# Group-norm sums with the squares as moving operand: four token tiles on four column groups of 32, then VectorE transposes

## The chip, the cores and the metric

The kernel runs on one core of one Trainium2 chip. The metric is the device time of one execution in microseconds (us), the median of several. Engines are named as in the profile: PE is TensorE's matmuls and PEld its weight loads, DVE is VectorE, ACT is ScalarE, POOL is GpSimd, SP is SyncE, which only issues DMAs here. A matmul has a stationary operand, which is loaded into the array first (PEld), and a moving operand, which streams through it (PE); the output has one partition for each column of the stationary operand.

## The reference, cut to what matters

One hybrid block over 512 tokens of width 1024: a dilated attention and a Mamba-2 mixer side by side, gates, an output projection, and an MLP, all float32. The change is in the grouped RMS norm at the end of the Mamba-2 mixer: 2048 channels in 8 groups of 256, and for each token and group the root mean square over the 256 channels.

```
y = y.reshape(b, s, SSM_INNER) * jax.nn.silu(z)
yg = y.reshape(b, s, SSM_GROUPS, SSM_INNER // SSM_GROUPS)
yg = yg * lax.rsqrt(jnp.mean(yg * yg, axis=-1, keepdims=True) + RMS_EPS)
y = yg.reshape(b, s, SSM_INNER) * norm_w
```

## The kernel before, in words

Tokens are 4 tiles of 128. The input projection, the attention, the Mamba-2 mixer, the output projection and the MLP follow each other; all large products run on PE as three passes of a split float32 (a high part, `hi` or `h`, and a rest, `lo` or `l`, in the type float32r), one matmul with 512 columns each. The weights come in units of 1 MB through two staging buffers (`ws`), and ACT and DVE split each unit into `wh` and `wl` (line 96 and line 99) before PE uses it.

The Mamba-2 mixer takes the 8 channel groups one after the other (`ssm_group`, line 768). Within a group the work is a chain of steps, and between the steps PE gets matmuls of the next units to do: the generator `ssm_group` yields, and the list `SSM_FILL` (line 46) says how many microseconds of projection work (x, B and C, z, and the projection of the group before, `sp`) go between two steps. Each matmul is kept in program order (`mm`, line 226), so the order on PE is that of the code. On DVE and ACT a part of the instructions is kept in order and the others are placed by the scheduler of the tile framework.

The part that the change touches is the end of a group. Channels lie on partitions and tokens along the free dimension, so `y` is two tiles (j = 0, 1) of 128 channels by 512 tokens. ACT squares both (line 841, the factor 1/sqrt(256) makes the sum a mean), DVE adds the two (line 844, into `sq[0]`), and then the sum over the 128 partitions is a matmul: for each token residue c the 128 tokens 4t + c (a column step of 4) are the stationary operand, and the first column of `ones` is the moving operand; the result is column c of `pn` with tokens on partitions (line 850). `rstd_of` adds epsilon on DVE (line 212, `rt`) and POOL raises to the power -1/2 (line 215). `rt` goes to DRAM and comes back spread over all partitions in token order (`rg`, lines 855 and 857, both issued from POOL), and DVE multiplies it in (line 864) to give `yt`, which the projection `sp` of the group needs.

On DVE the instruction `rt` stands among the instructions of the next group's convolution (lines 691 to 697: ACT makes `ch` from `psx`, DVE adds three taps with 511, 510 and 509 columns, ACT makes `ct`), and on ACT these are followed by the decays of the next group (`e` and `w`, lines 761 to 765) and by the split of the z weights (line 96).

Of the kernel before, what the change touches and what calls it, by code (L numbers as in the profile page):

```python
# [11 lines left out]
F32 = mybir.dt.float32  # L12
F32R = mybir.dt.float32r
AF = mybir.ActivationFunctionType
# [4 lines left out]
P = 128  # L19
T = 512  # L20
NT = 4
# [16 lines left out]
UC = 256  # L38
# [45 lines left out]
def hybrid_block(ctx: ExitStack, tc: tile.TileContext, a: dict):  # L84
    nc = tc.nc
    act, dve, pool, pe, sp = nc.scalar, nc.vector, nc.gpsimd, nc.tensor, nc.sync
# [8 lines left out]
    def split(src, hi, lo, eng=None, pinned=False, lo_pinned=False):  # L95
        ins = act.activation(hi, src, AF.Copy)  # L96
        if pinned:
            tc.keep_in_program_order(ins)
        ins = (eng or dve).tensor_tensor(lo, src, hi.bitcast(F32), op=ALU.subtract)  # L99
        if lo_pinned:  # L100
            tc.keep_in_program_order(ins)
# [107 lines left out]
    def rstd_of(dst, ms, ms2=None):  # L209

        if ms2 is None:
            dve.tensor_scalar(dst, ms, EPS, None, ALU.add)
        else:
            dve.tensor_scalar(dst, ms, ms2, EPS, ALU.add, ALU.add)
        pool.tensor_tensor(dst, dst, mhalf.broadcast_to(list(dst.shape)), op=ALU.pow)

    ones = const.tile([P, P], F32, name="ones")
# [5 lines left out]
    def pin(ins):  # L223
        return tc.keep_in_program_order(ins)

    def mm(*args, **kw):
        tc.keep_in_program_order(pe.matmul(*args, **kw))  # L227

    def tr(dst, src):
        tc.keep_in_program_order(pe.transpose(dst, src, ident))  # L230
# [4 lines left out]
    def three(ps, wh, wl, uh, ul, start, stop, w_moving=False):  # L235
        if w_moving:
            mm(ps, uh, wh, start=start, stop=False)
            mm(ps, uh, wl, start=False, stop=False)
            mm(ps, ul, wh, start=False, stop=stop)
        else:  # L240
            mm(ps, wh, uh, start=start, stop=False)
            mm(ps, wh, ul, start=False, stop=False)
            mm(ps, wl, uh, start=False, stop=stop)
# [14 lines left out]
    def abank(name):  # L258
        return psa.tile([P, T], F32, name=name, tag="a")
# [18 lines left out]
    with tc.tile_pool(name="start", bufs=1, reuse_waits="tile") as st:  # L278
# [163 lines left out]
        t = [vp.tile([P, GROUPS, NT, HG], F32, name=f"dt{j}") for j in range(4)]  # L442
# [185 lines left out]
    for key in ATT_UNITS:  # L628
        n, j = key[:-1], int(key[-1])
# [54 lines left out]
    sg = sctx.enter_context(tc.tile_pool(name="ssm", bufs=1, side="right", reuse_waits="tile"))  # L684
# [15 lines left out]
    def bc64(t, g, c0=0, c1=NT):  # L700
        v = t[:, g * 16 + c0 * HG : g * 16 + c1 * HG]
        return v.unsqueeze(2).broadcast_to([P, (c1 - c0) * HG, 64])

    def h64(ap_):
        return ap_.rearrange("p (q e) -> p q e", e=64)
# [62 lines left out]
    def ssm_group(g, sz):  # L768

        xs2 = [convs.pop((g, c)) for c in range(2)]  # L770
        w, e = ws_e.pop(g)

        xd = sg.tile([P, NT * UC], F32, name=f"xd{g}", tag="xd")
        for b in range(2):
            pt = abank(f"ptx{g}_{b}")
            for c2 in range(2):
                c = 2 * b + c2
                for j, xx in enumerate(xs2):
                    tr(pt[:, c2 * UC + j * P : c2 * UC + (j + 1) * P], xx[:, c * P : (c + 1) * P])
            dve.tensor_tensor(h64(xd[:, b * T : (b + 1) * T]), h64(pt), bc64(dtc, g, 2 * b, 2 * b + 2), op=ALU.mult)  # L780
        xs = sg.tile([P, 3 * UC], F32, name=f"xs{g}", tag="prev")
        dve.tensor_tensor(h64(xs), h64(xd[:, : 3 * UC]), bc64(ds_, g, 0, 3), op=ALU.mult)
        xsp = [sg.tile([P, 3 * UC], F32R, name=f"xs{n}{g}", tag=f"xs{n}") for n in "hl"]
        split(xs, *xsp)
        yield

        bt, ct = convs.pop((g, 2)), convs.pop((g, 3))
        pb = abank(f"pb{g}")
        for c in range(3):
            tr(pb[:, c * P : (c + 1) * P], bt[:, c * P : (c + 1) * P])  # L790
        bk = [sg.tile([P, TC], F32R, name=f"bk{n}{g}", tag=f"bk{n}") for n in "hl"]
        split(pb[:, :TC], *bk)
        pcb = abank(f"pcb{g}")
        for c in range(NT):
            cs = slice(c * P, (c + 1) * P)
            mm(pcb[:, cs], bt[:, cs], ct[:, cs], start=True, stop=True)
        cbm = sg.tile([P, NT, P], F32, name=f"cbm{g}", tag="cbm")
        dve.tensor_tensor(cbm, pcb.rearrange("p (c l) -> p c l", c=NT), tri.unsqueeze(1).broadcast_to([P, NT, P]),
                          op=ALU.mult)
        for c in range(NT):  # L800
            wv = w[:, c * HG : (c + 1) * HG, :]
            dve.tensor_tensor(wv, wv, cbm[:, c, :].unsqueeze(1).broadcast_to([P, HG, P]), op=ALU.mult)
        yield

        prev = sg.tile([P, 3, UC], F32, name=f"prev{g}", tag="prev")
        pst = [abank(f"pst{g}_{b}") for b in range(2)]
        for c in range(3):
            pv = pst[c // 2][:, (c % 2) * UC : (c % 2 + 1) * UC]
            bs, us = slice(c * P, (c + 1) * P), slice(c * UC, (c + 1) * UC)
            three(pv, bk[0][:, bs], bk[1][:, bs], xsp[0][:, us], xsp[1][:, us], True, True)  # L810
        with tc.high_priority(offset=200):
            act.activation(prev[:, 0, :], pst[0][:, 0:UC], AF.Copy)
            for c in (1, 2):
                pv = pst[c // 2][:, (c % 2) * UC : (c % 2 + 1) * UC]
                pin(dve.tensor_tensor(h64(prev[:, c, :]), h64(prev[:, c - 1, :]), bc64(cd, g, c, c + 1), op=ALU.mult))
                pin(dve.tensor_tensor(prev[:, c, :], prev[:, c, :], pv, op=ALU.add))
        while held:
            held.pop()()
        yield

        ys, sq = [], []
        pyds = [abank(f"pyd{g}_{j}") for j in range(2)]
        for j in range(2):
            for c in range(NT):
                for half in range(2):
                    h = 2 * j + half
                    mm(pyds[j][64 * half : 64 * half + 64, c * P : (c + 1) * P],
                       xd[:, c * UC + h * 64 : c * UC + (h + 1) * 64], w[:, c * HG + h, :], start=True, stop=True)
        for j in range(2):
            y = sg.tile([P, T], F32, name=f"y{g}_{j}", tag="y", bufs=2)  # L830
            dve.scalar_tensor_tensor(y, xs2[j], dskip[:, 2 * g + j : 2 * g + j + 1], pyds[j], op0=ALU.mult, op1=ALU.add)
            pyo = abank(f"pyo{g}_{j}")
            for c in range(1, NT):
                mm(pyo[:, (c - 1) * P : c * P], prev[:, c - 1, j * P : (j + 1) * P], ct[:, c * P : (c + 1) * P],
                   start=True, stop=True)
            t1 = sg.tile([P, TC], F32, name=f"t1{g}_{j}", tag="t1", bufs=2)
            dve.tensor_tensor(t1, pyo[:, :TC], e[:, j, :], op=ALU.mult)
            dve.tensor_tensor(y[:, P:], y[:, P:], t1, op=ALU.add)
            dve.scalar_tensor_tensor(y, y, 0.5, sz[j], op0=ALU.mult, op1=ALU.mult)
            q = sg.tile([P, T], F32, name=f"sq{g}_{j}", tag="sq", bufs=2)  # L840
            pin(act.activation(q, y, AF.Square, scale=1.0 / math.sqrt(UC)))
            ys.append(y)
            sq.append(q)
        dve.tensor_tensor(sq[0], sq[0], sq[1], op=ALU.add)
        yield

        pn = abank(f"pn{g}")
        by4 = sq[0].rearrange("p (t c) -> p c t", c=NT)
        for c in range(NT):
            mm(pn[:, c : c + 1], by4[:, c, :], ones[:, 0:1], start=True, stop=True)  # L850
        rt = sg.tile([P, NT], F32, name=f"rt{g}", tag="rt", bufs=2)
        rstd_of(rt, pn[:, :NT])

        row = dram.tile([P, NT], F32, name=f"rt_d{g}")
        pool.dma_start(row, rt)
        rstd = sg.tile([P, T], F32, name=f"rg{g}", tag="rg")
        pool.dma_start(rstd, row.rearrange("(o t) c -> o (t c)", o=1).broadcast_to([P, T]))
        if g + 1 < GROUPS:
            decays(g + 1)
        yield  # L860
        yield
        yt = yts[g] = [sg.tile([P, 2, T], F32R, name=f"yt{n}{g}", tag=f"yt{n}", bufs=1) for n in "hl"]
        for j in range(2):
            pin(dve.scalar_tensor_tensor(ys[j], ys[j], nw[:, 2 * g + j : 2 * g + j + 1], rstd,
                                         op0=ALU.mult, op1=ALU.mult))
            split(ys[j], yt[0][:, j, :], yt[1][:, j, :])
# [394 lines left out]
    j = last  # L1261
# [106 lines left out]
```

## Time and profile before

| | |
|---|---|
| time, median of 3 runs | 1097.21 us (1097.13 to 1097.43) |
| the profiled execution, its time | 1096.37 us |
| its span, first to last instruction | 1094.5 us |
| PE busy | 1083.4 us, 99% of the span |
| DVE, ACT, POOL busy | 730.9, 527.9, 72.0 us |
| mean granted TensorE clock | 0.998 of full speed |

A busy PE is an engine with a matmul in it, not one at its peak: matmuls overlap, and a row's length is longer than the step to the next row. What a block of matmuls costs is therefore read from the starts of the rows before and after it.

### The profile page before, as it was taken

How to read it: one execution, taken by the hardware profiler on the slowest of the kernel's cores; microseconds unless marked ns; L12 is line 12 of the kernel's file. 1: busy time of each engine (PE TensorE's matmuls, PEld its weight loads, DVE VectorE, ACT ScalarE, POOL GpSimd, SP SyncE). 2: the span in 40 equal slices, each digit the busy share in tenths (PEclk: the TensorE clock that was granted, in tenths of full speed). 3: DMA queues.
4: the chain of work that ended last, by engine and by line, in shares of the span. 5: the costliest groups of instructions: out<-in, count | busy, mean ns of one | idle time of the engine just before them, and what ended most of it. 6: DMA issues, size and time to landing. Idle time of an engine off the chain costs nothing.

```text
span 1094.5 us, 14714 instructions
## 1 busy us (share of the span) xinstructions
PE 1083.4 (99%) x5959; PEld 929.5 (85%) x5959; DVE 730.9 (67%) x1088; ACT 527.9 (48%) x921; POOL 72.0 (7%) x87
## 2 busy tenths in 40 slices
PE   9999999999999999999999999999999999999997
PEld 8988887778888888888888878889899998888886
DVE  6557666446776879696969695868677886243324
ACT  6256656435374645546373623443467666232322
POOL 3203122000000000000000000000000000000000
PEclk9999999999999999999999999999999999999999
DMA  8232112323333332323324222560233323333202
GB/s 278 81 116 78 55 63 68 106 68 106 116 87 119 84 125 78 125 82 121 112 92 150 86 82 88 191 192 1 78 116 116 102 93 135 116 118 113 80 37 78
DMA packets 87653, 113.06 MB, mean 103 GB/s; under 512 B 4624, under 2 KB 74768, under 8 KB 86560
## 3 DMA queue, kind: packets, MB, share of 16 engines
q1 hardware_dynamic: 85216, 101.01, 28.7%
q0 software_dynamic: 2224, 11.09, 3.0%
q8 instruction: 47, 0.77, 0.3%
q14 instruction: 22, 0.18, 0.1%
q10 hardware_dynamic: 144, 0.00, 0.0%
HBM read 109.92 MB, written 2.18 MB: 102 GB/s over the span
## 4 chain that ended last, share of the span: by engine, by line
PE 95%; DVE 2%; DMA 1%; issue 1%; ACT 1%; SPq 0%; POOLq 0%; POOL 0%; DVEq 0%; ACTq 0%
PE psd L227 15%; PE psx L227 8%; PE psz L227 8%; PE psbc L227 8%; PE pssp L227 7%; PE psuX L227 6%; PE psu L227 4%; PE psga L227 4%; PE psgs L227 4%; PE psk L227 3%; PE psq L227 3%; PE psuZ L227 3%; PE psv L227 3%; PE psap L227 3%; PE psp L227 2%; PE pso L227 2%
## 5 line engine op out<-in xcount | busy, mean ns | idle before, releaser
L227 PE MATMUL psd<-wl_dn,hh 128*128 128x512 f32 x240 | 93.5, 390 | 0.0
L227 PE MATMUL psd<-wh_dn,hh 128*128 128x512 f32 x240 | 93.5, 390 | 0.0
L227 PE MATMUL psd<-wh_dn,hl 128*128 128x512 f32 x240 | 93.5, 389 | 0.0
L99 DVE TENSOR_TENSOR hl<-hidden,hh 128x512 fp32r<-128x512 f32 x31 | 21.1, 692 | 71.3 <-ACT hh L96 71.3
L96 ACT ACTIVATE hh<-hidden 128x512 fp32r<-128x512 f32 x31 | 19.1, 628 | 91.8 <-PE psd L227 91.8
L227 PEld LDWEIGHTS psd<-wh_dn,hh 128*128 128x128 f32 x240 | 45.1, 188 | 9.4
L227 PEld LDWEIGHTS psd<-wl_dn,hh 128*128 128x128 f32 x240 | 45.1, 188 | 9.3
L227 PEld LDWEIGHTS psd<-wh_dn,hl 128*128 128x128 f32 x240 | 45.1, 188 | 9.3
L693 DVE SCALAR_TENSOR_TENSOR ch<-psx,cw,ch 128x511 f32<-128x511 f32 (+2 forms) x48 | 35.9, 747 | 23.0 <-ACT ch L691 22.3
L227 PE MATMUL psz<-uh,wh_z 128*128 128x512 f32 x128 | 51.1, 399 | 0.0
L227 PE MATMUL pssp<-yth,wh_sp 128*128 128x512 f32 x128 | 50.9, 398 | 0.0
L227 PE MATMUL psx<-uh,wl_x 128*128 128x512 f32 x128 | 50.1, 392 | 0.7 <-DVE wl_x L99 0.7
L227 PE MATMUL psx<-uh,wh_x 128*128 128x512 f32 x128 | 50.6, 395 | 0.0
L227 PE MATMUL pssp<-yth,wl_sp 128*128 128x512 f32 x128 | 50.2, 392 | 0.0
L227 PE MATMUL psz<-uh,wl_z 128*128 128x512 f32 x128 | 50.1, 391 | 0.0
L227 PE MATMUL pssp<-ytl,wh_sp 128*128 128x512 f32 x128 | 50.0, 391 | 0.0
L227 PE MATMUL psbc<-uh,wh_bc 128*128 128x512 f32 x128 | 50.0, 390 | 0.0
L227 PE MATMUL psz<-ul,wh_z 128*128 128x512 f32 x128 | 50.0, 390 | 0.0
L227 PE MATMUL psbc<-uh,wl_bc 128*128 128x512 f32 x128 | 49.9, 390 | 0.0
L227 PE MATMUL psbc<-ul,wh_bc 128*128 128x512 f32 x128 | 49.8, 389 | 0.0
L227 PE MATMUL psx<-ul,wh_x 128*128 128x512 f32 x128 | 49.8, 389 | 0.0
L696 ACT ACTIVATE ct<-ch 128x512 f32<-128x512 f32 x32 | 20.0, 626 | 52.1 <-DVE ch L693 52.1
(360 smaller groups left out, 3267.4 us busy)
## 6 DMA issues: line engine op xcount, KB each, us to landing
ws_up<-in_w_up_dram SPq DMA_DIRECT2D x16, 1024.0 KB, 5.5
ws_dn<-in_w_down_dram SPq DMA_DIRECT2D x15, 1024.0 KB, 5.0
ws_z<-in_w_in_dram SPq DMA_DIRECT2D x8, 1024.0 KB, 7.1
ws_x<-in_w_in_dram SPq DMA_DIRECT2D x8, 1024.0 KB, 5.2
w<-acs_d POOLq DMA_DIRECT2D x8, 1024.0 KB, 5.6
ws_bc<-in_w_in_dram SPq DMA_DIRECT2D x16, 512.0 KB, 4.7
ws_sp<-in_w_ssm_proj_dram SPq DMA_DIRECT2D x8, 1024.0 KB, 4.9
ws_ga<-in_w_in_dram SPq DMA_DIRECT2D x4, 1024.0 KB, 5.8
```

The costliest lines, as they stand in the source:

```text
L96: ins = act.activation(hi, src, AF.Copy)
L99: ins = (eng or dve).tensor_tensor(lo, src, hi.bitcast(F32), op=ALU.subtract)
L227: tc.keep_in_program_order(pe.matmul(*args, **kw))
L693: dve.scalar_tensor_tensor(h[:, d:], ps[:, : T - d], cw[:, ct, 3 - d : 4 - d], h[:, d:], op0=ALU.mult, op1=ALU.add)
L696: act.activation(t, h, AF.Tanh)
```

## The change

The squares are written in another order of tokens, and their sum over partitions is taken with the operands exchanged. ACT's square now reads `y` with a step of 4 tokens and writes `q` so that token 128j + 4p + b of the group lies at place 128j + 32b + p. Each matmul c now has 32 columns of `ones` as stationary operand and the 128 contiguous columns of token tile c as moving operand; its output is 32 equal rows, on partitions 32c to 32c + 31 of `pn`. The four matmuls thus use the four column groups of the array. A new DVE instruction transposes `pn` in squares of 32 by 32 into the new tile `pnt` (one more buffer of 512 bytes per partition in the pool `ssm`), so that partition 32c + p, square b, holds the mean of token 128c + 4p + b, and `rstd_of` reads the first column of each square. From `rt` on the layout is the same as before. The DMAs are the same.

```diff
-            pin(act.activation(q, y, AF.Square, scale=1.0 / math.sqrt(UC)))
+
+            pin(act.activation(q.rearrange("n (j b p) -> n j b p", j=NT, b=4),
+                               y.rearrange("n (j p b) -> n j b p", j=NT, b=4), AF.Square, scale=1.0 / math.sqrt(UC)))
...
         pn = abank(f"pn{g}")
-        by4 = sq[0].rearrange("p (t c) -> p c t", c=NT)
         for c in range(NT):
-            mm(pn[:, c : c + 1], by4[:, c, :], ones[:, 0:1], start=True, stop=True)
+            mm(pn[32 * c : 32 * c + 32, :P], ones[:, :32], sq[0][:, c * P : (c + 1) * P], start=True, stop=True)
+        pnt = sg.tile([P, 4, 32], F32, name=f"pnt{g}", tag="pnt")
+        dve.transpose(pnt.rearrange("p b q -> p (b q)"), pn[:, :P])
         rt = sg.tile([P, NT], F32, name=f"rt{g}", tag="rt", bufs=2)
-        rstd_of(rt, pn[:, :NT])
+        rstd_of(rt, pnt[:, :, 0])
```

On PE the place of the four matmuls is the same in all 8 groups; here the third group of channels, between matmuls of the x projection of the next one (`psx`). Before:

```order
L227 MATMUL psx_1_3489<-ul,wh_x_3354 128x512
L227 MATMUL psx_1_3489<-uh,wl_x_3355 128x512
L227 MATMUL pn_3496<-ones,sq_0_3404 128x1 x4
L227 MATMUL psx_1_3489<-uh,wh_x_3354 128x512
L227 MATMUL psx_1_3489<-ul,wh_x_3354 128x512
```

And now:

```order
L227 MATMUL psx_1_3493<-ul,wh_x_3358 128x512
L227 MATMUL psx_1_3493<-uh,wl_x_3359 128x512
L227 MATMUL pn_3500<-sq_0_3408,ones 32x128 x4
L227 MATMUL psx_1_3493<-uh,wh_x_3358 128x512
L227 MATMUL psx_1_3493<-ul,wh_x_3358 128x512
```

Nothing moved; only the form of the four is another. On DVE the same place, from the last step of `y` to the `ct` of the next group. Before:

```order
L839 SCALAR_TENSOR_TENSOR y_1_3406<-y_1_3406,sz_1_3312 128x512
L844 TENSOR_TENSOR sq_0_3404<-sq_0_3404,sq_1_3416 128x512
L693 SCALAR_TENSOR_TENSOR ch_3481<-psx_0_3456,cw,ch_3481 128x511
L212 TENSOR_SCALAR rt_3501<-pn_3496 128x4
L693 SCALAR_TENSOR_TENSOR ch_3481<-psx_0_3456,cw,ch_3481 128x510
L693 SCALAR_TENSOR_TENSOR ch_3481<-psx_0_3456,cw,ch_3481 128x509
L697 SCALAR_TENSOR_TENSOR ct_3486<-ct_3486,ch_3481 128x512
```

And now:

```order
L839 SCALAR_TENSOR_TENSOR y_1_3410<-y_1_3410,sz_1_3316 128x512
L846 TENSOR_TENSOR sq_0_3408<-sq_0_3408,sq_1_3420 128x512
L693 SCALAR_TENSOR_TENSOR ch_3485<-psx_0_3460,cw,ch_3485 128x511
L693 SCALAR_TENSOR_TENSOR ch_3485<-psx_0_3460,cw,ch_3485 128x510
L854 STREAM_TRANSPOSE pnt_3505<-pn_3500 128x128
L693 SCALAR_TENSOR_TENSOR ch_3485<-psx_0_3460,cw,ch_3485 128x509
L212 TENSOR_SCALAR rt_3507<-pnt_3505 128x4
L697 SCALAR_TENSOR_TENSOR ct_3490<-ct_3490,ch_3485 128x512
```

The instruction that waits for `pn` stands one place later: the tap with 510 columns now comes ahead of it, and the transpose between the taps with 510 and 509 columns. It is so in the third to the seventh group. Beside that, in the first group the mask product `cbm` (line 798) comes three places earlier on DVE, and one half of a split of x weights (line 96) four places earlier on ACT. POOL and SP have the same order as before.

## Rows read from the trace of the kernel before

**Rows 1.** The page: part 1 (busy time and share of the span), part 2 (the granted clock in 40 slices), part 4 (the chain that ended last, by engine).

```profile
PE 1083.4 (99%) x5959; PEld 929.5 (85%) x5959; DVE 730.9 (67%) x1088; ACT 527.9 (48%) x921; POOL 72.0 (7%) x87
...
PEclk9999999999999999999999999999999999999999
...
PE 95%; DVE 2%; DMA 1%; issue 1%; ACT 1%; SPq 0%; POOLq 0%; POOL 0%; DVEq 0%; ACTq 0%
```

**Rows 2.** Busy time by stretches, two whole groups, from one sum over partitions to the next; columns as in the head.

```profile
core 0: us, PE busy (x) PEld busy (x) DVE busy (x) ACT busy (x) POOL busy (x), PEclk, DMA share, GB/s
399.26:451.36 52.10, 52.10 (x273) 43.93 (x273) 42.53 (x63) 26.22 (x46) 2.72 (x4) 1.00 0.34 105
451.36:503.46 52.10, 52.10 (x273) 43.93 (x273) 42.53 (x63) 26.22 (x46) 2.73 (x4) 1.00 0.33 108
```

**Rows 3.** PE in order of time around one block of the sums (start us, length us, instruction; equal ones in a row are merged, the length is then that of the whole).

```profile
450.22 0.39 PE L227 MATMUL psx<-ul,wh_x 128*128 128x512 f32 x1
...
451.13 0.40 PE L227 MATMUL psx<-uh,wl_x 128*128 128x512 f32 x1
451.36 1.80 PE L227 MATMUL pn<-ones,sq 128*128 128x1 f32 x8
453.02 0.47 PE L227 MATMUL psx<-uh,wh_x 128*128 128x512 f32 x1
453.34 0.39 PE L227 MATMUL psx<-ul,wh_x 128*128 128x512 f32 x1
```

**Rows 4.** Groups of instructions by line and form (count, then busy us, mean ns of one, idle before).

```profile
L227 PEld LDWEIGHTS pn<-ones,sq 128*128 128x128 f32 x64 | 15.5, 324 | 0.3
L227 PEld LDWEIGHTS pcb<-ct,ct 128*128 128x128 f32 x64 | 7.8, 192 | 0.0
```

**Rows 5.** PE around 32 passes on two column groups of 64 (`pyd`, 16 matmuls), and eight passes on the whole array (`pcb`, 4 matmuls of the same 128 moving columns).

```profile
332.88 1.97 PE L227 MATMUL pyd<-w,xd 128*64 128x128 f32 x32
...
479.55 1.06 PE L227 MATMUL pcb<-ct,ct 128*128 128x128 f32 x8
```

**Rows 6.** The same two and the passes of `po` (the attention's values, also two column groups of 64) by form.

```profile
L227 PE MATMUL pyd<-w,xd 128*64 128x128 f32 x256 | 16.2, 277 | 0.8 <-DVE w L802 0.8
L227 PE MATMUL po<-pT,vtok 128*64 128x384 f32 x24 | 4.9, 486 | 0.0
L227 PE MATMUL po<-pT,vtok 128*64 128x256 f32 x24 | 3.6, 379 | 0.0
L227 PE MATMUL po<-pT,vtok 128*64 128x128 f32 x24 | 2.3, 273 | 0.0
L227 PE MATMUL pcb<-ct,ct 128*128 128x128 f32 x64 | 8.5, 275 | 0.0
```

**Rows 7.** PE around one block of `po` (8 matmuls, 16 passes of 512, 384, 128 and 256 columns, four of each), between matmuls on the whole array.

```profile
139.58 0.39 PE L227 MATMUL psq<-uh,wl_q 128*128 128x512 f32 x1
139.90 2.38 PE L227 MATMUL po<-pT,vtok 128*64 128x512 f32 x16
142.21 0.50 PE L227 MATMUL psq<-uh,wh_q 128*128 128x512 f32 x1
142.54 0.40 PE L227 MATMUL psq<-ul,wh_q 128*128 128x512 f32 x1
```

**Rows 8.** Groups by form: the squares on ACT, and a copy of 128 by 128 from PSUM on DVE.

```profile
L841 ACT ACTIVATE sq<-y 128x512 f32<-128x512 f32 x16 | 10.1, 632 | 70.5 <-DVE y L839 70.3
...
L635 DVE COPY acs<-pc 128x128 f32<-128x128 f32 x1 | 0.3, 290 | 2.9 <-PE pc L227 2.9
```

**Rows 9.** The weight loads of the sums of rows 3 on PE.

```profile
451.13 1.94 PEld L227 LDWEIGHTS pn<-ones,sq 128*128 128x128 f32 x8
```

**Rows 10.** DVE in order of time over the place of rows 3 (in brackets the idle time before and what ended it).

```profile
448.56 0.69 DVE L839 SCALAR_TENSOR_TENSOR y<-y,sz 128x512 f32<-128x512 f32 x1
449.95 0.69 DVE L844 TENSOR_TENSOR sq<-sq,sq 128x512 f32<-128x512 f32 x1 [0.70 <-ACT sq L841]
451.01 0.75 DVE L693 SCALAR_TENSOR_TENSOR ch<-psx,cw,ch 128x511 f32<-128x511 f32 x1 [0.37 <-ACT ch L691]
453.25 0.16 DVE L212 TENSOR_SCALAR rt<-pn 128x4 f32<-128x4 f32 x1 [1.50 <-PE pn L227]
453.33 1.52 DVE L693 SCALAR_TENSOR_TENSOR ch<-psx,cw,ch 128x510 f32<-128x510 f32 x2
```

**Rows 11.** ACT in order of time, from the square to the z weights' split.

```profile
449.29 0.63 ACT L841 ACTIVATE sq<-y 128x512 f32<-128x512 f32 x1 [2.75 <-DVE y L839]
...
454.95 0.63 ACT L696 ACTIVATE ct<-ch 128x512 f32<-128x512 f32 x1 [3.97 <-DVE ch L693]
455.49 1.87 ACT L761 ACTIVATE e<-w 64x384 f32<-64x384 f32 x4
457.38 0.40 ACT L764 ACTIVATE w<-w,acs 128x128 f32<-128x128 f32 x1
457.69 0.76 ACT L691 ACTIVATE ch<-psx,cb,cw 128x512 f32<-128x512 f32 x1
...
466.69 1.04 ACT L96 ACTIVATE wh_z<-ws_z 128x1024 fp32r<-128x1024 f32 x1
```

**Rows 12.** The second half of the z weights' rest on DVE in order of time, and the multiplication by `rg` after it.

```profile
467.76 1.22 DVE L99 TENSOR_TENSOR wl_z<-ws_z,wh_z 128x1024 fp32r<-128x1024 f32 x1 [0.67 <-ACT wh_z L96]
...
469.51 0.74 DVE L864 SCALAR_TENSOR_TENSOR y<-y,nw,rg 128x512 f32<-128x512 f32 x1
```

**Rows 13.** The weight load on PE that is the first to need the half of rows 12.

```profile
469.02 0.19 PEld L227 LDWEIGHTS psz<-uh,wl_z 128*128 128x128 f32 x1
```

**Rows 14.** POOL's issue of the spread of `rt` in order of time.

```profile
457.08 0.55 POOL L857 DMA_DIRECT2D rg<-rt_d  x1 [1.65 <-issue]
```

**Rows 15.** Its time from issue to landing, over all eight groups.

```profile
DMA to landing us min/median/max: 3.3/3.6/3.9
```

## The prediction

> **What bounds the kernel now.** I read the page first [rows 1]: PE has work in 99% of the span, the chain that ended last runs over PE for 95%, and the clock is at its upper level (2.4 GHz) in all slices. So the question is how long PE's own queue is, and where PE waits for something else. Then busy time by stretches [rows 2]: from one sum to the next a group takes 52.10 us, PE has no gap in it, DVE is busy 42.53 us (82%), ACT 26.22 us (50%). The reader is to see that time taken off PE's queue counts in full as long as DVE's and ACT's results still arrive in time, and that DVE has little to spare at single places.
>
> Next, PE in order of time around the sums [rows 3]. Matmuls with 512 columns start 0.2275 us apart (451.13 less 450.22, by 4). From the last one before the sums (451.13) to the second after them (453.34) are 2.21 us, where 2 x 0.2275 = 0.455 would do. The four sums, eight passes in the trace, thus cost 1.755 us per group, 14.04 us in all 8. With one moving column they stream nothing to speak of: the time is weight loads, and a load of the strided squares takes 324 ns, where one of 128 contiguous columns takes 192 [rows 4].
>
> **The change on PE.** It removes those 14.04 us and adds eight passes of 128 moving columns on column groups of 32. No row has groups of 32; two kinds have groups of 64, and I take the price from them.
>
> How many passes run at once: on the whole array the eight passes of `pcb` take 1.06 us less one length of 0.275, so 0.785 / 7 = 0.112 us each. The 32 passes of `pyd` with the same 128 columns take 1.97 - 0.277 = 1.69 us, by 31 is 0.055 us each [rows 5, 6]. Half the step at the same length of a pass: the two column groups run at once.
>
> What entering and leaving costs: the block of `po` takes 142.54 - 139.58 - 0.455 = 2.505 us [rows 7]. A pass grows by 486 - 379 = 107 ns, or 379 - 273 = 106 ns, per 128 columns [rows 6]. Its passes, two at once, are 2 x (512 + 384 + 128 + 256) = 2560 columns one after the other, 20 x 0.107 = 2.14 us. The rest, 0.365 us, is going into the split array and out of it, once per block.
>
> With four groups at once the new block is two rounds of 0.107 us and 0.365 us, together 0.58 us. It saves 1.755 - 0.58 = 1.175 us per group, 9.4 us in 8. If only two run at once it is four rounds, 0.79 us, saving 0.96 us, 7.7 us in all. If none do, eight rounds, 1.22 us, saving 0.53 us, 4.3 us. I take four at once, since `pyd` halves its step with nothing left over.
>
> The Trainium skill has a rule against this: TensorE: Matmul & The Clock Gate, Part 3, "The mechanism", says that matmuls start and end strictly in program order. The trace shows two passes of a matmul each; if those of one column group must follow each other and the next group may not pass them, four groups would overlap only where the second pass of one meets the first of the next. By that rule the sum would be about the case with two at once; by the halved step of `pyd` [rows 5] it is the case with four.
>
> **The square on ACT.** It is the same count of elements, read with a step of 16 bytes. Two squares per group, of 632 ns [rows 8]; the second is on the way to the sums. No row of ACT reads with such a step. The low bound is no change. The nearest row is the weight load with that very step, 132 ns more for 128 columns, so 1.03 ns per element and 0.53 us for 512 [rows 4]; I take this. Does PE see it? The sum of squares on DVE ends at 449.95 + 0.69 = 450.64 and the loads of the sums begin at 451.13 [rows 9, 10], 0.49 us later. Going into column groups moves the first pass further: at `po` it starts 139.90 - 139.58 = 0.32 us after the last matmul, where the step is otherwise 0.2275 [rows 7], so the slack is 0.58 us. Hence nothing at 0.53 us, and in the five groups with this order (the third to the seventh) 5 x (extra - 0.58) beyond. On ACT the second square delays `ch` (450.20, with 0.28 us idle before it), and DVE's first tap by about 0.2 us [rows 10, 11].
>
> SBUF — State Buffer of the Trainium skill, in its note on cachelines, says that a 4-byte read which meets a new 16-byte line each time pays a penalty. The trace agrees for the weight loads (324 against 192 ns [rows 4]); for ACT no run here shows it, and the page gives no figure.
>
> **The transpose on DVE.** Eight more instructions. The nearest row is the copy of 128 by 128 from PSUM, 290 ns [rows 8]; below I allow `rt`'s 160 ns, above the 690 ns of an instruction with 512 columns [rows 10]. I take 0.29 us, 2.3 us on DVE in all. Queued behind it on DVE are the tap with 509 columns, `rt` and `ct`, and ACT waits for these taps. So the place matters. Before, DVE stands 1.50 us waiting for `pn`, until 453.25, and two taps of 1.52 us together come behind it; ACT's `ct` (454.95, 3.97 us idle) follows, and from there ACT works without a gap up to the z weights [rows 10, 11]. Now the tap with 510 columns is done during the wait. The sums end 1.175 us earlier, at about 452.05; the taps with 511 and 510 columns are through at about 452.5 (452.7 with the longer square), the transpose at 452.8 to 453.0, the tap with 509 at 453.5 to 453.7. `ct` starts 1.25 to 1.4 us earlier than before.
>
> **What is late next.** PE reaches psz's low half 1.175 us earlier, and there the slack is 469.02 - (467.76 + 1.22) = 0.04 us [rows 12, 13]: the z weights' split must move forward by as much. Its chain on ACT begins with `ct` (1.25 us earlier) and with `ch` of psx at 457.69, which needs PE, itself 1.175 us earlier. So it follows, with next to nothing over. For the last hundredths, and for the first group's other order on DVE, I charge 0.06 us per group, 0.5 us in all. A transpose of 0.69 us would make that chain 0.2 to 0.3 us late in six groups, 1.5 us more. The spread of the result is covered: `rg` lands at 457.08 + 3.6 = 460.7, and DVE multiplies by it at 469.51 [rows 12, 14, 15]; two DVE instructions more ahead of it (0.29 + 0.75 us) do not reach that. POOL and SP issue the same DMAs in the same order.
>
> **Sum.** 9.4 - 0.5 = 8.9 us less. The profiled execution took 1096.37 us with a span of 1094.5 us and would take 1087.5; the median of the runs lies 0.84 us above it, so I predict 1097.21 - 8.9 = 1088.3 us.
>
> **Rivals.**
> 1. Two column groups at once, for which the rows themselves are the only evidence (no row has four). Saving 7.7 - 0.5 = 7.2 us: 1090.0 us.
> 2. The change doesn't do what it says: groups of 32 do not overlap, eight rounds. 4.3 - 0.5: 1093.4 us. Against it stand both blocks with groups of 64.
> 3. The gain turns into a wait for DVE or ACT: either the transpose takes 0.69 us (1.5 us more, 1089.8 us), or the square takes twice the taken surcharge, 1.06 us, and PE waits 0.48 us in five groups (2.4 us, 1090.7 us). For it speaks that two slacks are 0.04 and 0.58 us; against it that the tap now fills the wait.
> 4. Slower: the array is emptied at each change of column group instead of once per block. Then 0.365 us is paid four times, and with eight rounds the block costs 1.46 + 0.86 = 2.32 us, 0.56 us more than now in each group: 1097.2 + 4.5 = 1101.7 us. It decides from a block above 1.755 us. Against it: `pyd` changes between two groups all the time and shows no such gap.
>
> **Chances.** Forecast 0.58 (its own range 1087.0 to 1089.3), rival 1 0.20, rival 2 0.06, rival 3 0.11, rival 4 0.03; 0.02 for a gain lost wholly in waits, within 0.2%. A measurement of this kernel can tell 0.2%, 2.2 us, from no change. All cases but rival 4 and the last are faster by more: 0.95, 0.02, 0.03. The range 1086.8 to 1091.4 holds the forecast, rivals 1 and 3 and the bounds of square and transpose from below; rivals 2 and 4 are left out.
>
> **What would show it.** In PE's order the step from the last matmul before the sums to the second after them: 1.04 us for four at once, 1.25 for two, 1.68 for none, 2.8 for rival 4. Eight passes of `pn` with starts in two bunches of four. One group to the next in 50.9 us instead of 52.10. The square's mean (0.63 or 1.16 us), the transpose's (0.29 us), the idle of DVE before it, and PE's waits for `sq` and `wl_z`, which are to stay under 0.1 us each. The forecast is wrong if PE shows waits of several tenths there, or if the block's step is above 1.2 us.

## The result and the profile after

| | before | after |
|---|---|---|
| median | 1097.22 us (1097.13 to 1097.43, 4 runs) | 1087.28 us (1086.76 to 1087.56, 4 runs) |
| profiled execution; its span | 1096.37; 1094.5 us | 1087.34; 1085.6 us |

The ratio is 0.9909 (95% interval 0.9891 to 0.9926): 9.9 us less. Parts 1 and 4 of the page after [rows 1]:

```profile
PE 1074.3 (99%) x5959; PEld 915.7 (84%) x5959; DVE 732.2 (67%) x1096; ACT 535.5 (49%) x921; POOL 72.0 (7%) x87
...
PE 92%; DVE 4%; DMA 2%; ACT 1%; issue 1%; SPq 0%; POOL 0%; POOLq 0%; DVEq 0%; ACTq 0%
```

PE still has work in 99% of the span and lost 9.1 us of busy time. DVE gained 1.3 us and ACT 7.6 us, and the time fell all the same. The windows of two whole groups [rows 2]:

```profile
core 0: us, PE busy (x) PEld busy (x) DVE busy (x) ACT busy (x) POOL busy (x), PEclk, DMA share, GB/s
397.45:448.34 50.89, 50.89 (x273) 42.18 (x272) 42.62 (x64) 27.23 (x46) 2.72 (x4) 1.00 0.36 109
448.34:499.24 50.90, 50.90 (x273) 42.18 (x273) 42.64 (x64) 27.23 (x46) 2.72 (x4) 1.00 0.35 109
```

A group takes 50.893 us instead of 52.100, 1.207 less, and PE has no gap in it. Around one block, PE in order of time (start us, length us; equal rows merged) [rows 3]:

```profile
448.03 0.39 PE L227 MATMUL psx<-uh,wl_x 128*128 128x512 f32 x1
448.35 0.42 PE L227 MATMUL pn<-sq,ones 128*32 128x128 f32 x8
448.70 0.50 PE L227 MATMUL psx<-uh,wh_x 128*128 128x512 f32 x1
449.04 0.39 PE L227 MATMUL psx<-ul,wh_x 128*128 128x512 f32 x1
```

From the last matmul before the sums to the second after them are 449.04 - 448.03 = 1.01 us, where it was 2.21. Below, this stretch is called the step, and the step less the 0.455 us that it takes without sums is the block's cost: 1.755 us before, 0.556 now. Behind the merged row the eight starts lie, in ns: 0, 6, 13, 20, then 133, 140, 146, 153. Two bunches of four, 113 ns from the last start of one to the first of the other.

The square by form [rows 8], and then the answers by tile for `pnt` and `pn` (shortest, median, longest ns) [rows 4]:

```profile
L842 ACT ACTIVATE sq<-y 128x512 f32<-128x512 f32 x16 | 17.8, 1120 | 70.5 <-DVE y L839 70.4
```

```profile
L854 DVE STREAM_TRANSPOSE pnt<-pn x8: 304/306/317, 304.3 to 655.3; 128x128 f32<-128x128 f32 x8
```

```profile
L227 PEld LDWEIGHTS pn<-sq,ones x64: 106/108/110, 301.1 to 654.9; 128*32 128x32 f32 x64
L227 PE MATMUL pn<-sq,ones x64: 272/285/297, 301.1 to 655.0; 128*32 128x128 f32 x64
```

The square takes 1120 ns instead of 632; the transpose takes 306. DVE in order of time [rows 10]:

```profile
445.46 0.69 DVE L839 SCALAR_TENSOR_TENSOR y<-y,sz 128x512 f32<-128x512 f32 x1
447.33 0.69 DVE L846 TENSOR_TENSOR sq<-sq,sq 128x512 f32<-128x512 f32 x1 [1.18 <-ACT sq L842]
448.00 1.53 DVE L693 SCALAR_TENSOR_TENSOR ch<-psx,cw,ch 128x511 f32<-128x511 f32 x2
449.45 0.31 DVE L854 STREAM_TRANSPOSE pnt<-pn 128x128 f32<-128x128 f32 x1
449.68 0.71 DVE L693 SCALAR_TENSOR_TENSOR ch<-psx,cw,ch 128x509 f32<-128x509 f32 x1
450.31 0.16 DVE L212 TENSOR_SCALAR rt<-pnt 128x4 f32<-128x4 f32 x1
```

The wait of 1.50 us for `pn` is gone: two taps run in its place, and when the transpose comes, `pn` is done. Only in the last group does it still wait 0.48 us. And PE's loads there [rows 9]:

```profile
447.81 0.19 PEld L227 LDWEIGHTS psx<-uh,wl_x 128*128 128x128 f32 x1
448.35 0.16 PEld L227 LDWEIGHTS pn<-sq,ones 128*32 128x32 f32 x8 [0.35 <-DVE sq L846]
448.70 0.19 PEld L227 LDWEIGHTS psx<-uh,wh_x 128*128 128x128 f32 x1 [0.20 <-issue]
```

This row names a releaser, yet PE did not wait for the sum: the sum ended at 447.33 + 0.69 = 448.02, and the load began 0.33 us later. The 0.54 us between the loads are the same in the first group, where the sum ended 4.17 us before the load and the row names no releaser. Where PE's load does wait for the sum (squares made twice, below), it comes 0.05 us after the sum's end. So here the bracket names a semaphore and not the cause.

The z weights [rows 12, 13], DVE and then PE's load:

```profile
463.37 1.23 DVE L99 TENSOR_TENSOR wl_z<-ws_z,wh_z 128x1024 fp32r<-128x1024 f32 x1 [0.67 <-ACT wh_z L96]
```

```profile
464.71 0.19 PEld L227 LDWEIGHTS psz<-uh,wl_z 128*128 128x128 f32 x1
```

There 0.11 us are left (0.04 before). One new line stands among PE's waits, in the output projection:

```profile
PE ft L230 <- DVE sm L214: 0.3, 1, 0.3
```

Adding up the two profiles by the starts of PE's stages: the seven steps from group to group save 8.44 us and the eighth group, up to the output projection, 1.29: 9.73 us. Against that stand 0.60 us before the first sums and 0.45 us at `ft`; from `ft` to the end 0.26 us are saved. That gives the 8.9 us between the spans. Of the 0.60 us 0.53 lie before the first `psq` (50.30 us from the start before, 50.83 after), ahead of every changed instruction. What the wait at `ft` hangs on, the section on the hardware shows. The profiled execution of before was also 0.85 us under its median, while that of after lies on its own.

### The profile page after: what moved, and what is told of

The parts are those of the page before. It is cut to its first block, busy times and chain, and to the rows that moved or that the text cites. A ratio compares the mean times of both kernels' runs of the same rounds, so it can differ in the third digit from the quotient of the medians.

```text
span 1085.6 us, 14723 instructions
## 1 busy us (share of the span) xinstructions
PE 1074.3 (99%) x5959; PEld 915.7 (84%) x5959; DVE 732.2 (67%) x1096; ACT 535.5 (49%) x921; POOL 72.0 (7%) x87
## 4 chain that ended last, share of the span: by engine, by line
PE 92%; DVE 4%; DMA 2%; ACT 1%; issue 1%; SPq 0%; POOL 0%; POOLq 0%; DVEq 0%; ACTq 0%
PE psd L227 16%; PE psx L227 8%; PE psz L227 8%; PE psbc L227 8%; PE pssp L227 7%; PE psuX L227 6%; PE psu L227 4%; PE psga L227 4%; PE psgs L227 4%; PE psk L227 3%; PE psq L227 3%; PE psuZ L227 3%; PE psv L227 3%; PE psap L227 3%; PE psuY L227 1%; PE pq L227 1%
## 5 line engine op out<-in xcount | busy, mean ns | idle before, releaser
L842 ACT ACTIVATE sq<-y 128x512 f32<-128x512 f32 x16 | 17.8, 1120 | 70.5 <-DVE y L839 70.4
```

The costliest lines, as they stand in the source:

```text
L842: pin(act.activation(q.rearrange("n (j b p) -> n j b p", j=NT, b=4), y.rearrange("n (j p b) -> n j b p", j=NT, b=4), AF.Square, scale=1.0 ...
```

## The experiments

All take the changed kernel (or, where said, the one before) and change the end of the group. Before's median was 1097.0 us beside each of them (1097.02, 1097.02 and 1097.00 in the three comparisons).

**Four matmuls on one column group.**

```diff
-            mm(pn[32 * c : 32 * c + 32, :P], ones[:, :32], sq[0][:, c * P : (c + 1) * P], start=True, stop=True)
+            mm(pn[0:32, c * P : (c + 1) * P], ones[:, :32], sq[0][:, c * P : (c + 1) * P], start=True, stop=True)
```

(The transpose is then 32 x 512, the root 32 x 16, and the DMA writes the same order.)

> The four sums all go to column group 0, side by side in the free dimension, so that nothing can overlap; the transpose and the DMA of rt take the other layout. Theory (the gain comes from four column groups at once): eight rounds of 0.107 us in place of two, so the step from the last matmul before the sums to the second after them goes from 1.01 to 1.65 us, a group from 50.89 to 51.53 us, and the time is 1087.3 + 8 x 0.64 = 1092.4 us. Rival (the gain comes only from the operands' exchange and the contiguous columns, not from the groups): step 1.0 to 1.1 us, time 1087 to 1088 us. If the cost of entering and leaving the split array is what counts, it is paid here too, since the array is still split.

Measured: 1091.39 us (1090.91 to 1091.78), ratio 0.9948 (0.9934 to 0.9963). PE:

```profile
449.29 0.39 PE L227 MATMUL psx<-uh,wl_x 128*128 128x512 f32 x1
449.61 1.06 PE L227 MATMUL pn<-sq,ones 128*32 128x128 f32 x8
450.60 0.50 PE L227 MATMUL psx<-uh,wh_x 128*128 128x512 f32 x1
450.93 0.40 PE L227 MATMUL psx<-ul,wh_x 128*128 128x512 f32 x1
```

Step 1.65 us, period 51.446, passes 0.109 us apart. The time came out 1.0 us under the expected 1092.4; the step is as expected. Of the 1.0 us some 0.5 lie outside the step, where a group takes 0.08 us less than in the changed kernel (see the last group of experiments).

**Two column groups.** The same with `pn[32 * (c % 2) : ...]`.

> The four sums alternate between column groups 0 and 1. Theory: four rounds, step 1.225 us, a group 51.11 us, time 1089.0 us. By the rule of strict order (the second pass of one group holds up the next group's first) the same overlap would be had as with four groups, so the step would be that of the changed kernel, 1.01 us, 1087.3 us.

Measured: 1088.79 us (1088.75 to 1089.53), ratio 0.9926 (0.9912 to 0.9941); step 1.22 us, period 51.133, four pairs of starts 6 or 7 ns apart and 102 ns or more from pair to pair.

```profile
448.34 0.39 PE L227 MATMUL psx<-uh,wl_x 128*128 128x512 f32 x1
448.65 0.63 PE L227 MATMUL pn<-sq,ones 128*32 128x128 f32 x8
...
449.56 0.40 PE L227 MATMUL psx<-ul,wh_x 128*128 128x512 f32 x1
```

So one, two and four groups give eight, four and two rounds of 0.11 us, and a remainder that is nearly the same: 1.65 - 0.455 - 8 x 0.109 = 0.32, 1.22 - 0.455 - 4 x 0.109 = 0.33, 1.01 - 0.455 - 2 x 0.109 = 0.34 us. Overlap only at the seam between one matmul's second pass and the next one's first would have made two groups cost what four cost.

**The old operands without the step in the loads.** The kernel before, with squares written residue by residue, so that each load reads 128 contiguous columns.

```diff
-            pin(act.activation(q, y, AF.Square, scale=1.0 / math.sqrt(UC)))
+            pin(act.activation(q.rearrange("n (c t) -> n c t", c=NT), y.rearrange("n (t c) -> n c t", c=NT),
+                               AF.Square, scale=1.0 / math.sqrt(UC)))
...
-            mm(pn[:, c : c + 1], by4[:, c, :], ones[:, 0:1], start=True, stop=True)
+            mm(pn[:, c : c + 1], sq[0][:, c * P : (c + 1) * P], ones[:, 0:1], start=True, stop=True)
```

> The operands as in the kernel before (squares stationary, one column of ones moving, whole array), but the square writes each token residue contiguously, so that the weight loads have no step. Theory (the old block was dear because the loads read with a step of 16 bytes): loads at the 0.11 us of other passes on 128 contiguous columns, eight of them 0.9 us, step 1.35 us, a group 51.25 us, time 1097.2 - 6.9 = 1090.3 us. Rival (a load that has no matmul to hide behind costs 0.233 us whatever its step): step 2.2 us, a group 52.1 us, time 1097 us.

Measured: 1089.75 us (1089.32 to 1090.11), ratio 0.9933 (0.9919 to 0.9948); step 1.36 us, period 51.253. PE, and its loads by form:

```profile
449.00 0.40 PE L227 MATMUL psx<-uh,wl_x 128*128 128x512 f32 x1
449.24 0.95 PE L227 MATMUL pn<-ones,sq 128*128 128x1 f32 x8
...
450.36 0.39 PE L227 MATMUL psx<-ul,wh_x 128*128 128x512 f32 x1
```

```profile
L227 PEld LDWEIGHTS pn<-ones,sq 128*128 128x128 f32 x64 | 8.4, 191 | 0.6
```

The loads fell from 324 to 191 ns, and with them the block from 1.755 to 0.90 us. That is 0.85 of the 1.20 us that the whole change saves per group; exchanging the operands and four column groups bring the other 0.35. The exchange alone would cost time: with one column group the step is 1.65 us, 0.29 us more than here. The square takes 1119 ns here too, so this gain also rests on an ACT that has time for it, and the time is used up: in the third to the seventh group PE's first load comes 0.05 us after the end of the sum and 0.27 us after the load before it, where 0.23 is usual.

**Each square made twice** (the second overwrites the first with the same values).

```diff
-            pin(act.activation(q.rearrange("n (j b p) -> n j b p", j=NT, b=4),
...
+            for _ in range(2):
+                pin(act.activation(q.rearrange("n (j b p) -> n j b p", j=NT, b=4),
...
```

> The changed kernel with each square made twice into the same tile, which adds 1.12 us to the way to the sums. In the changed kernel the sum of squares on DVE ends 0.33 us before the sums' first load. Theory (the strided square is hidden, with 0.33 us left): PE waits 0.8 us for the sums in the third to seventh group and some tenths in the last, none in the first two; 4 to 5 us in all, time 1091.3 to 1092.3 us. Rival (PE's place leaves the square more room than the rows show): under 1 us, 1087 to 1088 us.

Measured: 1098.21 us (1096.38 to 1099.36, 10 runs), ratio 1.001 (1.000 to 1.002), period 52.48 us. The direction was right and the size was not. The chain, in the waits, on ACT and on DVE:

```profile
PE pn L227 <- DVE sq L848: 9.6, 6, 2.1
```

```profile
448.76 1.11 ACT L843 ACTIVATE sq<-y 128x512 f32<-128x512 f32 x1 [0.88 <-DVE y L839]
449.77 0.76 ACT L691 ACTIVATE ch<-psx,cb,cw 128x512 f32<-128x512 f32 x1
450.44 1.10 ACT L843 ACTIVATE sq<-y 128x512 f32<-128x512 f32 x1
```

```profile
448.05 0.68 DVE L839 SCALAR_TENSOR_TENSOR y<-y,sz 128x512 f32<-128x512 f32 x1
450.57 0.75 DVE L693 SCALAR_TENSOR_TENSOR ch<-psx,cw,ch 128x511 f32<-128x511 f32 x1 [1.84 <-ACT ch L691]
451.57 0.69 DVE L848 TENSOR_TENSOR sq<-sq,sq 128x512 f32<-128x512 f32 x1 [0.25 <-ACT sq L843]
```

The scheduler put `ch` between the two squares. From the end of `y` to the start of the sum are 451.57 - 448.73 = 2.84 us, where it was 447.33 - 446.15 = 1.18: 1.0 us for the square and 0.67 for `ch`. What it shows is how thin the cover is: an instruction of 1.1 us more on ACT cost PE 1.6 us in each of the fourth to the seventh group (2.2 in the third, 1.5 in the last) and ate the whole gain.

**The square reads in order and writes with the step.**

```diff
-            pin(act.activation(q.rearrange("n (j b p) -> n j b p", j=NT, b=4),
+            pin(act.activation(q.rearrange("n (j b p) -> n j p b", j=NT, b=4),
-                               y.rearrange("n (j p b) -> n j b p", j=NT, b=4), AF.Square, scale=1.0 / math.sqrt(UC)))
+                               y.rearrange("n (j p b) -> n j p b", j=NT, b=4), AF.Square, scale=1.0 / math.sqrt(UC)))
```

> The square reads y in order and writes its result with the step (128 bytes from one element to the next), where the changed kernel reads with a step of 16 bytes and writes in order; everything else, the order on each engine too, is the changed kernel's. If only a stepped read makes ScalarE slow, the square takes 0.63 to 0.70 us as in the kernel before; if a step on either side does, it takes about 1.1 us again. The time is that of the changed kernel to within 0.5 us by both (1086.8 to 1087.8), since the sum of the squares ends 0.33 us before TensorE's load in the changed kernel and the 0.47 us of a shorter square only add to that room; period 50.89 us, step over the block 1.01 us. A rival, that TensorE's load does wait for the sum (the 0.35 us that the trace puts before it), has the step fall to about 0.7 us and the time to about 1084.8.

Measured: 1086.91 us (1086.86 to 1087.02), ratio 0.9908 (0.9891 to 0.9926); step and period as in the changed kernel.

```profile
L842 ACT ACTIVATE sq<-y 128x512 f32<-128x512 f32 x16 | 18.4, 1168 | 70.5 <-DVE y L839 70.3
```

A step on the writing side costs as much. The rival, that PE waits for the sum, gets no test from this run, since the square did not become shorter. The first two groups of the changed kernel settle it: there the sum ends 4.2 and 6.0 us before the load, and the loads are 0.54 us apart all the same.

**One matmul with all 128 columns of ones**, in float32 and in float32r. Here it is the kernel before, with its plain square, that is changed; the way through DRAM falls away.

```diff
-        for c in range(NT):
-            mm(pn[:, c : c + 1], by4[:, c, :], ones[:, 0:1], start=True, stop=True)
...
+        mm(pn, ones, sq[0], start=True, stop=True)
...
+        dve.tensor_scalar(rstd, pn, EPS, None, ALU.add)
+        pool.tensor_tensor(rstd, rstd, mhalf.broadcast_to([P, T]), op=ALU.pow)
```

> One float32 matmul with all 128 columns of ones and 512 moving columns puts each token's sum on every partition: no transpose, no round trip through DRAM, VectorE adds the constant and GpSimd takes the root over 128x512, and the square is the plain one. If passes in one column range follow one another whatever the width, the block is two passes of 512 columns: 2 x 0.227 + about 0.34 in and out = 0.79, so the step is 0.79 + 0.45 = 1.2 to 1.33 us where the changed kernel has 1.01; period 51.1 to 51.2, time 1089 to 1090 as long as GpSimd's root over 128x512 (no row shows it) takes under 10 us. If what costs is the number of loads and matmuls (8 against 2), the step falls under 0.8 us and the time to about 1085.5.

> As the kernel with one float32 matmul, but the sum of the squares and the ones are in float32r, so that TensorE makes one pass of 512 columns (the sum's operands are rounded to that type). If the 0.34 us in and out of the block belongs to any change of operand, the step is 0.227 + 0.11 + 0.34 = 0.68 us, period 50.56, time 1084.6. If it belongs to the float32 passes alone, the step is that of one more matmul in the row, 2 x 0.227 = 0.45 us, period 50.33, time 1082.8. If VectorE's and GpSimd's longer work (128x512 each in place of 128x4) or the sum ends after TensorE gets there, TensorE waits at pn or at the next group's psz and the time stays over 1086.

Measured: 1619.46 us (ratio 1.4764, 1.4738 to 1.4790) and 1626.02 us (1.4820, 1.4796 to 1.4843). As times both are misses, from one row of the first:

```profile
L853 POOL TENSOR_TENSOR rg<-rg,mhalf 128x512 f32<-128x512 f32 x8 | 655.6, 81947 | 136.6 <-DVE rg L852 136.6
```

The root over 128 x 512 takes 82 us, not under 10. It could have been worked out: before, 128 x 1 takes 546 ns and 128 x 4 takes 1033 on the same line 215, 0.16 us per column, so 512 columns are 83 us. PE's block can still be read, in the first of the two:

```profile
651.42 0.39 PE L227 MATMUL psx<-uh,wl_x 128*128 128x512 f32 x1
651.65 1.02 PE L227 MATMUL pn<-sq,ones 128*128 128x512 f32 x2
652.11 0.79 PE L227 MATMUL psx<-uh,wh_x 128*128 128x512 f32 x1
652.74 0.39 PE L227 MATMUL psx<-ul,wh_x 128*128 128x512 f32 x1
```

The step is 1.31 us, the cost 0.858: two passes of 0.429, with nothing for going in and out. That the step lies in the expected 1.2 to 1.33 us is luck: a pass was put at 0.227, and 0.34 were for going in and out. In float32r the step is 0.69 us and the cost 0.236, one pass. (Both steps of that expectation were added up too short. "One more matmul in the row" is 3 x 0.227 = 0.68 us, not 0.45; with 0.34 in and out it is some 1.03, not 0.68. So the 0.69 speak for nothing in and out.)

**Wide and narrow, float32r and float32.** To use that without the long root: one matmul of 512 moving columns, its first 32 partitions transposed and sent on as with one column group. The first `mm` is the wide kernel's, the second the narrow one's; the third is the narrow kernel in float32, which keeps the sum in `sq[0]`.

```diff
+    ones_r = const.tile([P, P], F32R, name="ones_r")
+    act.activation(ones_r, ones, AF.Copy)
...
+        sq_r = sg.tile([P, T], F32R, name=f"sqr{g}", tag="sqr")
+        dve.tensor_tensor(sq_r, sq[0], sq[1], op=ALU.add)
...
+        mm(pn, ones_r, sq_r, start=True, stop=True)
+        mm(pn[0:32, :], ones_r[:, :32], sq_r, start=True, stop=True)
+        mm(pn[0:32, :], ones[:, :32], sq[0], start=True, stop=True)
```

> One float32r matmul with all 128 columns of ones and 512 moving columns (the sum of the squares rounded to that type), of which the first 32 partitions are transposed and sent through DRAM as in the kernel with one column group; square as in the changed kernel, GpSimd's root over 32x16. The kernel with GpSimd's long root showed for this matmul a block of 0.236 us with no gap in or out, so the step is 0.69 us, the period 50.57 and the time about 1084.7 (8 x 0.32 us under the changed kernel). Rival: the sum of the squares is late. In the changed kernel it ends 0.33 us before TensorE's load, which comes 0.31 us late by the gap on the way in; without that gap about 0.02 us is left, and if the order of the squares moves by one place on ScalarE or VectorE, TensorE waits 0.1 to 0.7 us per group: 1085.5 to 1090.

> As the kernel with one wide float32r matmul, but with 32 columns of ones, so that one column range of the array is used. If the 0.34 us in and out of the changed kernel's block belongs to the change of tile shape (128 columns to 32 and back), the block is 0.236 + 0.34 = 0.58, the step 1.03 us, the period 50.91 and the time about 1087.4. If it belongs to the number of loads or to float32, there is no gap here: step 0.69 us, period 50.57, time about 1084.7, as with the wide one.

> One float32 matmul with 32 columns of ones and 512 moving columns (two passes) in place of the four with 128 moving columns of the kernel with one column group; the rest is that kernel's. By the tile shape: 0.858 for the two passes (as measured with 128 columns) + 0.34 = 1.20, step 1.65 us, period 51.45, time about 1091.4, as that kernel. By the number of loads (2 against 8): no gap, step 1.31 us, period 51.11, time about 1088.7.

| one matmul, 512 moving columns | step | passes | in and out | time | ratio |
|---|---|---|---|---|---|
| float32, 128 columns of ones | 1.31 us | 2 x 0.429 | 0 | (long root) | |
| float32, 32 columns | 1.63 us | 2 x 0.429 | 0.32 | 1091.38 us | 0.9949 (0.9934 to 0.9964) |
| float32r, 128 columns | 0.69 us | 0.24 | 0 | 1083.92 us | 0.9882 (0.9865 to 0.9898) |
| float32r, 32 columns | 0.69 us | 0.23 | 0 | 1083.52 us | 0.9877 (0.9862 to 0.9891) |

PE with 32 columns of ones, in float32 and in float32r:

```profile
449.24 0.39 PE L227 MATMUL psx<-uh,wl_x 128*128 128x512 f32 x1
449.56 1.04 PE L227 MATMUL pn<-sq,ones 128*32 128x512 f32 x2
450.53 0.50 PE L227 MATMUL psx<-uh,wh_x 128*128 128x512 f32 x1
450.87 0.39 PE L227 MATMUL psx<-ul,wh_x 128*128 128x512 f32 x1
```

```profile
446.41 0.39 PE L230 MATMUL psx<-uh,wl_x 128*128 128x512 f32 x1
446.63 0.39 PE L230 MATMUL pn<-sqr,ones_r 128*32 128x512 f32 x1
446.86 0.40 PE L230 MATMUL psx<-uh,wh_x 128*128 128x512 f32 x1
447.10 0.39 PE L230 MATMUL psx<-ul,wh_x 128*128 128x512 f32 x1
```

Neither of the two theories holds alone: the 0.32 to 0.34 us are paid only where a float32 matmul meets a narrow stationary operand. (The old operands without the step fit in: float32, 128 columns, eight passes of 0.112 us make 0.90 with nothing over.) Both float32r kernels beat the changed kernel, by 3.4 and 3.8 us; the difference between them is within their runs. 2.6 us of it are the block, 8 x 0.32. The period with 32 columns is 50.50 us, where the shorter block alone would give 50.57. Outside the step a group takes some 0.08 us less than in the changed kernel in the middle groups of all four kernels whose root is 32 x 16 (one column group and the last three), in small portions along PE's queue; the cause stays open. The expected rival, that the sum comes late, shows in small: in the third to the seventh group the load comes 0.05 us after the end of the sum in both float32r kernels, and the step grows by more than 0.01 us only in the third, to 0.79 us (wide) and 0.72 (narrow). In exchange the sum of the squares is rounded before PE reads it.

## Why the prediction was right

1088.3 us was forecast and 1087.28 measured, inside the likeliest case's own range. Step by step:

- *The old block costs 1.755 us per group.* Yes: loads without their step took 0.85 us off it by themselves.
- *Four groups at once, two rounds of 0.107 us.* Yes: two bunches of four, and the row of one, two and four groups with 0.109 us a round. Rival 1 (two at once) has its own kernel now: 1088.79 us where 1090.0 was given. Rivals 2 and 4 fall with the same rows.
- *0.365 us in and out, taken from `po`.* Measured 0.34, and 0.32 to 0.34 for one, two or four groups. That "the split array" costs this is shown for float32 alone: a narrow float32r block pays nothing.
- *The square, 0.53 us more.* 0.49, and hidden. The price came from a weight load on PE; why it fits an instruction on ACT no run shows, so the near hit may be luck. That PE's slack is 0.58 us was too small. It is the load that needs the sum, and by the loads the way in moves it by 0.54 - 0.23 = 0.31 us, where I had read 0.09 off the matmuls' starts. So the old 0.49 us grow to 0.80, and 0.33 are left, of which 0.05 pass between a sum's end and a load that waits for it.
- *The transpose, 0.29 us, hidden behind DVE's vanished wait.* 0.306, and the taps stand as predicted. Rival 3 did not come.
- *The z weights follow.* Yes, with 0.11 us of room.
- *0.5 us for couplings.* This is the term that was mis-sized: nothing of it was paid. The groups saved 9.73 us, against 9.4 less 0.5. That the spans of the two profiled executions differ by the forecast 8.9 us all the same is luck: that difference holds the scatter before `psq` and at `ft`.

Against the forecast the prediction set a rule: the Trainium skill, TensorE: Matmul & The Clock Gate, Part 3, "The mechanism", has matmuls start and end in program order. Here four starts fall within 20 ns and the next four 113 ns later. Passes on one column group come 0.109 us apart, so a bunch of four must be on four groups, and the second pass of a float32 matmul does not hold back the next column group. What failed is that condition, which the prediction had added. The page's rule itself is neither broken nor confirmed: the trace does not say which record of a bunch belongs to which matmul.

## What to carry to other kernels

Look at the access pattern of a small matmul's stationary operand before its count: most of this gain was a load with a step of 16 bytes, and it moved to an engine with time to spare. Column groups overlapped here in proportion to their number (one, two, four), but a float32 block on a narrow operand pays 0.34 us once; one float32r matmul with 512 columns costs less than all of it, if the rounding is allowed. When cover is counted to a waiting engine, count to its load, and count GpSimd's power by its columns, 0.16 us each here.

## What was not expected of the hardware

- **In and out belongs to type and width together.** Of the four kernels in the table only float32 with 32 columns has it, 0.54 us between loads where it is 0.23 otherwise, as long as the load does not wait for the sum. The Trainium skill, TensorEngine Tiling (Array Packing), Key Properties, says that changing the tiling mode drains the engine. The float32 runs fit that (0.32 to 0.34 us per block). The narrow float32r block costs what the wide one does (0.23 and 0.24 us); whether the array changes its mode there no run shows, since the rows give only the number of columns in use.
- **ACT and steps.** 512 float32 values take 632 ns in order, 1120 when read with a step of 16 bytes, 1168 when written with a step of 128.
- **The transpose on DVE goes by columns.** 128 x 128 takes 306 ns, 64 x 256 takes 432 and 32 x 512 takes 703: the same number of elements.
- **The wait at `ft` follows the landing of a DMA of weights.** The weight load for `ft` needs `fn` from DVE, whose chain stands behind the split of the up weights, and ACT's half of that starts when a DMA lands:

```profile
725.29 1.92 ACT L96 ACTIVATE wh_up<-ws_up 128x2048 fp32r<-128x2048 f32 x1 [4.75 <-DMA ws_up<-in_w_up_dram]
```

```profile
716.61 1.92 ACT L96 ACTIVATE wh_up<-ws_up 128x2048 fp32r<-128x2048 f32 x1 [4.97 <-DMA ws_up<-in_w_up_dram]
```

The first is before, the second after. Counted from the first matmul of the output projection, this row starts at 25.48 us before and 25.92 after, and the load for `ft` at 35.38 and 35.83. In the kernel with contiguous loads it is 25.50 and 35.41, with one column group 25.88 and 35.80, with squares made twice 25.73 and 35.64, and in the kernel that writes with the step, whose order on every engine is the changed kernel's, 25.59 and 35.50. `ft` follows this row by 9.9 us each time, and the row differs by 0.33 us between two kernels of one order on every engine. The row follows the landing: its DMA is issued at 20.07 us before and 20.21 after and lands 5.30 and 5.60 us later, and the DMA ahead of it, issued at 13.37 us in both, lands 5.42 and 5.63 us later. That the change adds something to it can't be excluded with one profile of each. The start of the first `psq` scatters too, from 50.30 to 50.98 us among these profiles; why, was not looked into.
